# A Mamba-2 mixer on one core: the gates' SiLU ordered behind a group's exponentials, the samples' states in three spread steps

## The chip, the cores and the metric

The kernel runs on one core of a Trainium2 chip. The metric is device time in microseconds (us): the median of three runs before the change is 1595.83 us (1595.36 to 1596.58). A core has five engines that work side by side and wait for one another through semaphores: PE (matrix products, with PEld for its weight loads), DVE (vector), ACT (functions such as exp, SiLU and square root, and scaled copies), POOL (a second, slower vector engine) and SP, which here issues all DMA transfers. Each engine works through its own list of instructions in order: whatever waits at the head of a list holds up all that stands behind it.

## The reference

One step of a two-layer decoder for a prompt of 512 tokens and, with the same weights, 8 samples of 8 tokens each. The kernel carries both as 512 + 64 = 576 columns. Layer 0 is a convolution and window attention mixer, layer 1 a Mamba-2 mixer; each is followed by a gated feed-forward network (FFN). What matters here is the second mixer:

```python
z, xbc, dt = jnp.split(h @ w_in, [D_INNER, D_INNER + SSM_CONV_DIM], axis=-1)
xbc = jax.nn.silu(causal_dwconv(padded, conv_w, conv_b))
...
dt = jax.nn.softplus(dt.astype(jnp.float32) + dt_bias.astype(jnp.float32))
a = -jnp.exp(a_log.astype(jnp.float32))
y, new_ssm = ssd_scan(xs, dt, a, bm, cm, ssm_hist)
y = (y + d_skip[:, None] * xs).reshape(b, t, D_INNER) * jax.nn.silu(z)
y = rmsnorm(y.reshape(b, t, SSM_GROUPS, gs), gn_g.reshape(SSM_GROUPS, gs)).reshape(b, t, D_INNER)
return y @ w_out, new_conv, new_ssm
```

`ssd_scan` works on 32 heads in 4 groups of 8. Within a chunk of 128 tokens it weighs pairs of tokens by exponentials of differences of a running sum (the "decays"), and from chunk to chunk it carries a state. The samples start from given states (`state_ssm`): each of the 8 samples adds what its state gives to its outputs (`y_off`), and returns its state, decayed and with its own tokens added (`h_final`).

## The kernel before

The program is written as straight code over tiles of 128 rows. A scheduler that runs when the kernel is built sets the order on each engine; it may move instructions past one another where the data allow it. Two calls bind it: `keep_in_program_order(m)` keeps a matmul right where the program has it behind the one before, and `issue_after(ins)` keeps what is issued inside its block behind `ins` on the same engine.

**Large products.** Every product with a weight is made of three (L160, L161, L162): weights and activations are split into a high and a low part, and high x high, low x high and high x low are summed. A matmul has 288 columns, half of 576. Weights come by DMA into `wr` (3 buffers, 512 KB each, L141), ACT copies the high part `wh` (L150), DVE subtracts to get the low part `wl` (L151). Results go to PSUM tiles `mm`, of which there are 3 in this mixer.

**The second mixer** (`mix1`) runs `ssd(g)` for groups g = 0 to 3. `ssd` is a generator: at each of its `yield`s the function `run` may emit one item of the list `side`, so that large products lie between the group's own small ones. For g = 0 the side list holds the projections of z for this group (`z_units`, results to `zs`) and of B and C of the next. For g = 1 and 2 it holds the output projection of group g - 1 (`ot`, 8 tiles, activations `yh`/`yl`, in the text "y products") and then z. For g = 3 it holds z first, then four of the eight output tiles of group 2; the other four follow the group.

**Inside a group.** For each chunk c a state is made: a product `pst` (L990), summed into `hst` on DVE (L995, L996); the last goes out (L1000, `out_ssm_p`). Then, for each t = 0 to 3 (two heads each): `carried(t)` loads `ea2` (L1030) and takes its exponential (L1031); `decays` loads `acb` (256 KB, L1017), takes four ReLUs and one Exp on ACT (L1021, L1022), and a product with `cbm` on DVE (L1023); `outputs(t)` runs eight products into `yp` (L1047) from the two `acb`, and two DVE operations (L1051, L1052). After t = 1 and t = 3 comes `samples(bh)` for four samples: it loads four states `h0` (256 KB each, L1060), runs four products `pyo` (L1064), each with 32 output rows, into one PSUM tile, and one DVE operation makes `yo` (L1066); then for each sample a product `pst` (L1071), a scaling of `h0` on POOL (L1072), a sum on DVE (L1075) and the store (L1076). At the group's end `ysp` (L1095, L1100) joins the samples' parts.

**The gate.** `gate(g)` applies SiLU to the four `zs` tiles (L1119), multiplies, sums squares, takes 1/sqrt by way of PE, ACT and DVE (`rstd`, L182 to L197), scales (L1127) and splits into `yh`/`yl` (L170, L171), which the next group's side list, or after g = 3 the last output projection, uses. Exp, SiLU and Sqrt need different tables on ACT; where the next function's table isn't loaded, an ACT_TABLE_LOAD stands ahead of it.

**Memory slots.** Nearly all tiles come from one list of equal slots (48, and 9 more from the first FFN on). `S` takes the slot that was freed first in the program, `free` appends. A tile's DMA therefore waits until the last user of that slot is done, whoever that is. `zs` takes four slots at the start of a group, `prev` (the y tiles of the group before) are freed after `gate`, and `self.h` (16 slots) at the end of the mixer.

In the profile and in the lists of instructions, numbers at the end of a tile's name are left out: `h<-in_h` is `h0` read from memory, `ea` is `ea2`, `x` and `b` in a row of `pst` are `x3` and `b3`.

Of the kernel before, what the change touches and what calls it, by code (L numbers as in the profile page):

```python
# [22 lines left out]
HALF = (slice(0, HB), slice(HB, T))  # L23
# [26 lines left out]

class Builder:
    NSLOT = 48
    EXTRA = 9

    def __init__(self, nc, tc, d, stack):
        self.nc, self.tc, self.d = nc, tc, d
# [718 lines left out]
    def mix1(self):  # L775
        nc, d = self.nc, self.d
# [53 lines left out]
        W = 160  # L830
# [14 lines left out]
        nc.vector.scalar_tensor_tensor(e, v, -1.0, v, op0=MUL, op1=MAX)  # L845
        nc.scalar.activation(e, e, AF.Exp, scale=-1.0)
# [67 lines left out]
        def ssd(g):  # L914
# [18 lines left out]
            b3 = []  # L933
# [80 lines left out]
            def decays(r):  # L1014

                acb = self.S("acb", NP)
                nc.sync.dma_start(acb, acd[8 * g + r, 0:NP].partition_broadcast(P))  # L1017
                for c in range(4):
                    cs = slice(c * P, (c + 1) * P)
                    o = c * 32 + 8 * g + r  # L1020
                    nc.scalar.activation(acb[:, cs], acb[:, cs], AF.Relu, bias=ac[:, o:o + 1], scale=-1.0)  # L1021
                nc.scalar.activation(acb, acb, AF.Exp, scale=-1.0)  # L1022
                nc.vector.tensor_tensor(acb, acb, cbm[:, :NP], op=MUL)  # L1023
                return acb

            def carried(t):

                ea2 = self.S("ea2", NP - P)
                for hh in range(2):
                    nc.sync.dma_start(ea2[hh * 64:hh * 64 + 64, :], acd[8 * g + 2 * t + hh, P:NP].partition_broadcast(64))  # L1030
                nc.scalar.activation(ea2, ea2, AF.Exp)  # L1031
                py = self.ps("py")
                for c in range(1, 4):
                    nc.tensor.matmul(py[:, (c - 1) * P:c * P], H[c - 1][:, t * P:(t + 1) * P], cf[:, c * P:(c + 1) * P],
                                     start=True, stop=True)
                nc.vector.tensor_tensor(ea2, ea2, py[:, 0:NP - P], op=MUL)
                return ea2

            def outputs(t, ea2, pair):

                yp = self.ps("yp", "yp")
                for c in range(4):
                    cs = slice(c * P, (c + 1) * P)
                    for hh in (1, 0):
                        r = 2 * t + hh
                        rows, ch = slice(hh * 64, hh * 64 + 64), slice(r * 64, r * 64 + 64)
                        m = nc.tensor.matmul(yp[rows, cs], xdt[c][:, ch], pair[hh][:, cs], start=True, stop=True)  # L1047
# [7 lines left out]
            def samples(bh):  # L1055

                h0 = []
                for b4 in range(4):
                    h0.append(self.S("h0", NP))
                    nc.sync.dma_start(h0[-1], d["h0"][4 * bh + b4, g])  # L1060
                pyo = self.ps("pyo", "pyo")
                for b4 in range(4):
                    b = 4 * bh + b4
                    nc.tensor.matmul(pyo[b4 * 32:b4 * 32 + 32, :], cf[:, NP + 8 * b:NP + 8 * b + 32], h0[b4], start=True, stop=True)  # L1064
                o = self.S("yo", NP)
                nc.vector.tensor_tensor(hp(o), hp(pyo), eax[:, bh * 32 + 8 * g:bh * 32 + 8 * g + 8].unsqueeze(2).broadcast_to([P, 8, 64]), op=MUL)  # L1066
                yo.append(o)
                for b4 in range(4):
                    b = 4 * bh + b4
                    pst = self.ps("pst")  # L1070
                    nc.tensor.matmul(pst, b3[bh][:, b4 * P:(b4 + 1) * P], x3[bh], start=True, stop=True)  # L1071
                    nc.gpsimd.tensor_tensor(hp(h0[b4]), hp(h0[b4]),  # L1072
                                            cds[:, b * 32 + 8 * g:b * 32 + 8 * g + 8].unsqueeze(2).broadcast_to([P, 8, 64]),
                                            op=MUL)
                    nc.vector.tensor_tensor(h0[b4], h0[b4], pst, op=ADD)  # L1075
                    nc.sync.dma_start(d["ssm_s"][b, g], h0[b4])  # L1076
                    self.free(h0[b4])
# [26 lines left out]
            self.free(bf, cf, cbm, xdt, H, es, yo)  # L1104

        def z_units(g):
            zss[g] = [self.S("zs") for _ in range(4)]

            def evac(t):
                return lambda half, p: nc.scalar.activation(zss[g][t][:, HALF[half]], p[:, :HB], AF.Copy)  # L1110
            return [(d["w_in_o"][4 * g + t], P, evac(t)) for t in range(4)]

        def gate(g, yv):

            zs = zss.pop(g)
            ssq, rs = self.S("gssq"), self.S("grs")
            ys = [self.pair("y") for _ in range(4)]
            for t in range(4):
                nc.scalar.activation(zs[t], zs[t], AF.Silu)  # L1119
# [22 lines left out]
        def single(units):  # L1142
            return [lambda u=u: self.units([u], 1) for u in units]

        ys = None
        for g in range(4):
            xs = xss[g]
            side = []
            zu = z_units(g)
            if g:  # L1150
                ws = {}
                prev, srcs = ys, [d["w_out_o"][g - 1, c] for c in range(4)]

# [8 lines left out]
                side = single(zu) + ot[:4] if g == 3 else ot + single(zu)  # L1162
# [7 lines left out]
            if g:  # L1170
                self.free(prev)
# [180 lines left out]
```

## Time and profile before

| | us |
|---|---|
| median of three runs | 1595.83 (1595.36 to 1596.58) |
| profiled execution, its own time | 1596.65 |
| its span, first to last instruction | 1594.9 |
| PE busy in the span | 1560.2 (98%) |
| DVE busy | 999.7 (63%) |
| ACT busy | 656.1 (41%) |
| POOL busy | 149.4 (9%) |

The page's "busy" of PE is the time in which at least one matmul is in flight; matmuls overlap, so a row's duration (0.29 us for a matmul of 288 columns) is longer than the distance to the next one's start. For what a matmul costs in a dense stream the distance between starts is read. "Idle before" is the time an engine stood still ahead of an instruction, with the engine or DMA that ended it. The clock column (PEclk) is the TensorE clock that was granted, as a share of full speed.

### The profile page before, as it was taken

The numbers are of one execution on the slowest core, as the hardware profiler recorded it, in microseconds if no ns is written. First come the engines' busy times: TensorE is split into PE (matmuls) and PEld (weight loads), VectorE is DVE, ScalarE is ACT, GpSimd is POOL, SyncE is SP. The second block draws the span as 40 slices with busy tenths as digits, with TensorE's granted clock in tenths as the row PEclk, the third lists the DMA queues.
The fourth block names the chain that finished last, engine by engine and source line by source line (L and its number), as shares of the span: only waits on it lengthen the run. The fifth ranks groups of instructions, "written<-read, shape, count | busy, mean of one in ns | idle before, by whom it ended". The sixth has DMA issues, their size and how long they took to land.

```text
span 1594.9 us, 28738 instructions
## 1 busy us (share of the span) xinstructions
PE 1560.2 (98%) x11709; PEld 1479.2 (93%) x11709; DVE 999.7 (63%) x1750; ACT 656.1 (41%) x1210; POOL 149.4 (9%) x362
## 2 busy tenths in 40 slices
PE   8999999999999999999999999999999999999999
PEld 8976799999999999998987987998899999999999
DVE  7958486663564464678885686676776643663552
ACT  6257363321232222479654655556443221221220
POOL 0026001000000000101202101101110000000000
PEclk9999999999999999999999999999999999999999
DMA  7514223222222222226245226235222232223222
GB/s 229 117 54 102 70 83 101 80 81 92 80 77 84 93 80 75 74 82 203 74 120 186 74 81 195 89 96 182 81 89 84 80 91 83 80 73 97 83 82 76
DMA packets 69841, 157.60 MB, mean 99 GB/s; under 512 B 20158, under 2 KB 24510, under 8 KB 69710
## 3 DMA queue, kind: packets, MB, share of 16 engines
q1 hardware_dynamic: 69710, 155.77, 31.9%
q8 instruction: 92, 1.51, 0.4%
q14 instruction: 39, 0.32, 0.1%
HBM read 140.54 MB, written 15.21 MB: 98 GB/s over the span
## 4 chain that ended last, share of the span: by engine, by line
PE 82%; DVE 7%; ACT 4%; DMA 4%; issue 1%; POOL 1%; SPq 0%; ACTq 0%; DVEq 0%; POOLq 0%
PE mm L160 24%; PE mm L161 24%; PE mm L162 24%; DMA acb<-acd 2%; DVE cconv L801 1%; PE mm L559 1%; PE yp L1047 1%; DMA h<-in_h 1%; PE pyo L1064 1%; PE pt L182 1%; DVE ca L436 1%; ACT wh L150 1%; DVE wl L151 1%; ACT acb L1021 1%; PE pr L193 1%
## 5 line engine op out<-in xcount | busy, mean ns | idle before, releaser
L160 PE MATMUL mm<-hh,wh 128*128 128x288 f32 (+1 forms) x2288 | 682.8, 299 | 8.4 <-ACT wh L150 7.7
L161 PE MATMUL mm<-hl,wh 128*128 128x288 f32 (+1 forms) x2288 | 678.6, 297 | 0.0
L162 PE MATMUL mm<-hh,wl 128*128 128x288 f32 x2288 | 677.6, 296 | 0.0
L150 ACT ACTIVATE wh<-wr 128x1024 fp32r<-128x1024 f32 (+1 forms) x215 | 223.4, 1039 | 541.0 <-PE mm L161 273.6
L160 PEld LDWEIGHTS mm<-hh,wh 128*128 128x128 f32 (+1 forms) x2288 | 429.8, 188 | 14.9 <-ACT wh L150 7.9
L161 PEld LDWEIGHTS mm<-hl,wh 128*128 128x128 f32 (+1 forms) x2288 | 430.2, 188 | 5.6 <-issue 3.8
L162 PEld LDWEIGHTS mm<-hh,wl 128*128 128x128 f32 x2288 | 430.7, 188 | 2.7 <-issue 1.3
L151 DVE TENSOR_TENSOR wl<-wr,wh 128x1024 fp32r<-128x1024 f32 (+1 forms) x215 | 259.2, 1206 | 77.5 <-ACT wh L150 77.3
L160 PE MATMUL mm<-yh,wh 128*128 128x288 f32 x960 | 286.8, 300 | 2.2 <-ACT yh L170 2.2
L161 PE MATMUL mm<-yl,wh 128*128 128x288 f32 x960 | 288.2, 300 | 0.1
L162 PE MATMUL mm<-yh,wl 128*128 128x288 f32 x960 | 284.8, 297 | 1.4 <-DVE wl L151 1.4
L162 PEld LDWEIGHTS mm<-yh,wl 128*128 128x128 f32 x960 | 181.6, 189 | 6.1 <-issue 4.1
L161 PEld LDWEIGHTS mm<-yl,wh 128*128 128x128 f32 x960 | 181.9, 189 | 5.3 <-issue 4.0
L160 PEld LDWEIGHTS mm<-yh,wh 128*128 128x128 f32 x960 | 181.5, 189 | 4.4 <-ACT yh L170 2.6
L259 DVE TENSOR_TENSOR x<-x,mm 128x288 f32<-128x288 f32 x192 | 85.4, 450 | 157.4 <-PE mm L162 157.2
L304 DVE TENSOR_TENSOR gbuf<-mm,rs 128x224 f32<-128x224 f32 x44 | 17.2, 391 | 108.0 <-PE mm L162 108.0
L315 ACT ACTIVATE gsilu<-gconv,par 128x512 f32<-128x512 f32 x44 | 31.8, 723 | 115.5 <-DVE gconv L312 115.5
L312 DVE SCALAR_TENSOR_TENSOR gconv<-gbuf,par,gconv 128x592 f32<-128x592 f32 x88 | 73.1, 831 | 1.5
L325 DVE TENSOR_TENSOR gsilu<-mm,gsilu 128x288 f32<-128x288 f32 x88 | 40.0, 454 | 49.7 <-PE mm L162 49.7
L801 DVE SCALAR_TENSOR_TENSOR cconv<-cbuf,par,cconv 128x600 f32<-128x600 f32 x72 | 61.5, 857 | 13.0 <-ACT cconv L799 12.0
L307 POOL COPY fpo<-gbuf 128x2 f32<-128x2 f32 x44 | 12.4, 281 | 497.6 <-DVE gbuf L304 497.6
L1072 POOL TENSOR_TENSOR h<-h,cds 128x512 f32<-128x512 f32 x32 | 36.7, 1166 | 186.5 <-PE pyo L1064 167.8
(306 smaller groups left out, 1640.9 us busy)
## 6 DMA issues: line engine op xcount, KB each, us to landing
wr<-in_w_gate SPq DMA_DIRECT2D x44, 512.0 KB, 3.3
wr<-in_w_up SPq DMA_DIRECT2D x44, 512.0 KB, 3.3
wr<-in_w_in_o SPq DMA_DIRECT2D x40, 512.0 KB, 3.5
wr<-in_w_down SPq DMA_DIRECT2D x32, 448.0 KB, 3.4
wr<-in_w_down SPq DMA_DIRECT2D x16, 512.0 KB, 3.5
acb<-acd SPq DMA_DIRECT2D x32, 256.0 KB, 3.9
h<-in_h SPq DMA_DIRECT2D x32, 256.0 KB, 3.5
out_ssm_s<-h SPq DMA_DIRECT2D x32, 256.0 KB, 2.1
```

What stands on the lines that cost most here:

```text
L150: nc.scalar.activation(hi[:, :n], raw[:, :n], AF.Copy)
L151: nc.vector.tensor_tensor(lo[:, :n], raw[:, :n], hi[:, :n].bitcast(F32), op=SUB)
L160: nc.tensor.matmul(out, hi[:, ws], xh[:, sl], start=i == 0, stop=False)
L161: nc.tensor.matmul(out, hi[:, ws], xl[:, sl], start=False, stop=False)
L162: nc.tensor.matmul(out, lo[:, ws], xh[:, sl], start=False, stop=i == n - 1)
L259: nc.vector.tensor_tensor(self.x[m][:, sl], self.x[m][:, sl], p[:, :HB], op=ADD)
L304: nc.vector.tensor_tensor(g[:, 290:514], p[:, 0:224], rs[:, HB:NP], op=MUL)
L312: nc.vector.scalar_tensor_tensor(cv[:, :592], g[:, k:592 + k], w(k), cv[:, :592], op0=MUL, op1=ADD)
L315: nc.scalar.activation(sl[:, :NP], cv[:, :NP], AF.Silu, bias=b)
L325: nc.vector.tensor_tensor(sl[:, HALF[half]], p[:, :HB], sl[:, HALF[half]], op=MUL)
L801: nc.vector.scalar_tensor_tensor(cv[:, :600], g[:, k:600 + k], w(k), cv[:, :600], op0=MUL, op1=ADD)
L1072: nc.gpsimd.tensor_tensor(hp(h0[b4]), hp(h0[b4]), cds[:, b * 32 + 8 * g:b * 32 + 8 * g + 8].unsqueeze(2).broadcast_to([P, 8, 64]), op=MUL)
```

## The change

Four edits, all but the first three lines in `mix1`.

- **Samples in three steps.** `samples` becomes `load(bh)` (the four loads of `h0`), `begin(bh)` (the four `pyo` products, kept in one run, the last sample's first; all four scalings on POOL; `yo`) and `finish(bh, behind)` (the four `pst`, kept behind the last `yp` product of the t at hand, the sums and the stores). `load(0)` stands ahead of t = 0, `begin(0)` after t = 0, `finish(0)` after t = 1, `load(1)` right behind it, `begin(1)` after t = 2, `finish(1)` after t = 3.
- **SiLU behind the exponentials.** The gate's four SiLU are issued behind the group's last Exp of `decays`.
- **Slots.** 11 extra slots for 9 (five small tiles of the softplus become slots that are freed); `zs` takes its slot when its first half is written; `prev` is freed when the eighth output tile is issued; in the last group `self.h` is freed as soon as the z projections have used it.

```diff
-    EXTRA = 9
+    EXTRA = 11
...
-        v = self.Z("sp_v", W, bufs=1)
+        v = self.S("sp_v", W)
...
-        e, z, z2, q = (self.Z(n_, W, bufs=1) for n_ in ("sp_e", "sp_z", "sp_z2", "sp_q"))
+        e, z, z2, q = (self.S(n_, W) for n_ in ("sp_e", "sp_z", "sp_z2", "sp_q"))
...
+        self.free(v, e, z, z2, q)
...
-                nc.scalar.activation(acb, acb, AF.Exp, scale=-1.0)
+                self.last_exp = nc.scalar.activation(acb, acb, AF.Exp, scale=-1.0).ins
...
+                return m.ins
+
+            h0 = {}
+
+            def load(bh):
+                h0[bh] = []
                 for b4 in range(4):
-                    h0.append(self.S("h0", NP))
-                    nc.sync.dma_start(h0[-1], d["h0"][4 * bh + b4, g])
+                    h0[bh].append(self.S("h0", NP))
+                    nc.sync.dma_start(h0[bh][b4], d["h0"][4 * bh + b4, g])
+
+            def begin(bh):
                 pyo = self.ps("pyo", "pyo")
+                for b4 in (3, 2, 1, 0):
+                    b = 4 * bh + b4
+                    m = nc.tensor.matmul(pyo[b4 * 32:b4 * 32 + 32, :], cf[:, NP + 8 * b:NP + 8 * b + 32], h0[bh][b4],
+                                         start=True, stop=True)
+                    if b4 < 3:
+                        self.tc.keep_in_program_order(m)
                 for b4 in range(4):
                     b = 4 * bh + b4
-                    nc.tensor.matmul(pyo[b4 * 32:b4 * 32 + 32, :], cf[:, NP + 8 * b:NP + 8 * b + 32], h0[b4], start=True, stop=True)
+                    nc.gpsimd.tensor_tensor(hp(h0[bh][b4]), hp(h0[bh][b4]),
+                                            cds[:, b * 32 + 8 * g:b * 32 + 8 * g + 8].unsqueeze(2).broadcast_to([P, 8, 64]),
+                                            op=MUL)
...
+            def finish(bh, behind):
                 for b4 in range(4):
                     b = 4 * bh + b4
                     pst = self.ps("pst")
-                    nc.tensor.matmul(pst, b3[bh][:, b4 * P:(b4 + 1) * P], x3[bh], start=True, stop=True)
...
+                    with self.tc.issue_after(behind):
+                        nc.tensor.matmul(pst, b3[bh][:, b4 * P:(b4 + 1) * P], x3[bh], start=True, stop=True)
+                    nc.vector.tensor_tensor(h0[bh][b4], h0[bh][b4], pst, op=ADD)
+                    nc.sync.dma_start(d["ssm_s"][b, g], h0[bh][b4])
+                    self.free(h0[bh][b4])
...
             for t in range(4):
+                if t == 0:
+                    load(0)
                 ea2 = carried(t)
...
-                outputs(t, ea2, pair)
+                last = outputs(t, ea2, pair)
                 yield
                 if t % 2:
-                    yield from samples(t // 2)
+                    yield from finish(t // 2, last)
+                    if t == 1:
+                        load(1)
+                else:
+                    begin(t // 2)
...
-            for t in range(4):
-                nc.scalar.activation(zs[t], zs[t], AF.Silu)
+            with self.tc.issue_after(self.last_exp):
+                for t in range(4):
+                    nc.scalar.activation(zs[t], zs[t], AF.Silu)
...
+                    if m == 7:
+                        self.free(prev)
...
+                def last_h():
+                    self.free(self.h)
+                    self.h = []
+                side = single(zu) + [last_h] + ot[:4] if g == 3 else ot + single(zu)
```

The scheduler then makes new lists. On PE and ACT they are the same as before up to the mixer's first group and again in the second FFN; in the FFNs POOL's small fills and copies stand in a somewhat different order. What lies between is ordered anew. Line numbers behind L833 move: L1064 becomes L1070, L1071 becomes L1089, L1047 L1048, L1022 L1023, L1119 L1145, L1060 L1063, L1017 L1018, L1000 L1001, L1005 L1006.

**PE, the second group's t = 3 before, with its second four samples.** Before, two of the four `pyo` stand here and the other two 27 and 34 rows further on, each alone among large products:

```order
L1064 MATMUL pyo<-h_9493,cfm 32x512
L1064 MATMUL pyo<-h_9495,cfm 32x512
L1071 MATMUL pst<-x_8868,b_8849 128x512 x2
L160 MATMUL mm<-hh,wh 128x288
L161 MATMUL mm<-hl,wh 128x288
L162 MATMUL mm<-hh,wl 128x288
L1047 MATMUL yp<-acb,xdt 64x128 x8
L1071 MATMUL pst<-x_8868,b_8849 128x512
```

Now, the same four samples' products ahead of the `yp` of t = 2:

```order
L162 MATMUL mm<-hh,wl 128x288
L1070 MATMUL pyo<-h_9307,cfm 32x512
L1070 MATMUL pyo<-h_9305,cfm 32x512
L1070 MATMUL pyo<-h_9303,cfm 32x512
L1070 MATMUL pyo<-h_9301,cfm 32x512
L1048 MATMUL yp<-acb,xdt 64x128 x8
L1035 MATMUL py<-cfm,hst 128x128 x3
```

All eight sets of four `pyo` now stand as one run. Before, only the two of the first group did: the list had 18 runs in all. The eight `yp` products of a t, split as 1 and 7 at two places before, are whole everywhere. In the last group, the large y products that are left between the last `yp` and the end of the output tiles are 112 now; they were 64.

**SP, the second group from its exponentials' loads on.** Before:

```order
L1005 DMA es<-acd 64x8x64
L1030 DMA ea_9074<-acd 64x384 x2
L1017 DMA acb<-acd 128x512 x2
L1030 DMA ea_9172<-acd 64x384 x2
L1017 DMA acb<-acd 128x512
L1000 DMA out_ssm_p<-hst 128x512
L141 DMA wr<-in_w_in_o 128x1024
L1017 DMA acb<-acd 128x512
L1060 DMA h_9244<-in_h 128x512
L1060 DMA h_9242<-in_h 128x512
```

Now, from the third load of a sample's state (two more stand right ahead of it):

```order
L1063 DMA h_9076<-in_h 128x512
L1031 DMA ea_9078<-acd 64x384 x2
L1018 DMA acb<-acd 128x512
L1006 DMA es<-acd 64x8x64
L1063 DMA h_9070<-in_h 128x512
L141 DMA wr<-in_w_in_o 128x1024
L1018 DMA acb<-acd 128x512
L1031 DMA ea_9187<-acd 64x384 x2
L1018 DMA acb<-acd 128x512
L1063 DMA h_9301<-in_h 128x512
L1001 DMA out_ssm_p<-hst 128x512
L1018 DMA acb<-acd 128x512
```

The states' loads moved ahead of the decays' loads, and those of the second four samples to either side of the `acb` that stands behind the store of the chunk's state. That `acb` (the fourth of the group) takes the slot of the stored `hst` in both lists and so waits for that store to land.

**ACT, the third group's last exponentials.** Before:

```order
L1022 ACTIVATE acb<-acb 128x512
L1119 ACT_TABLE_LOAD
L1119 ACTIVATE zs<-zs 128x576
L1021 ACTIVATE acb<-acb,ac 128x128 x4
L1110 ACTIVATE zs<-mm 128x288
L1022 ACT_TABLE_LOAD
L1022 ACTIVATE acb<-acb 128x512
L1110 ACTIVATE zs<-mm 128x288
```

Now:

```order
L1022 ACTIVATE acb<-acb,ac 128x128 x2
L1134 ACTIVATE zs<-mm 128x288
L1022 ACTIVATE acb<-acb,ac 128x128 x2
L150 ACTIVATE wh<-wr 128x1024
L1023 ACTIVATE acb<-acb 128x512
L1145 ACT_TABLE_LOAD
L1145 ACTIVATE zs<-zs 128x576
L1134 ACTIVATE zs<-mm 128x288
```

The two table loads between the last two Exp are gone; one stands behind the last Exp. Over the program there are 36 table loads, 49 before.

More of the change, by code (lines that the diff above doesn't have):

```diff
@@ L1053, in outputs @@
                 self.free(pair, ea2)
-            def samples(bh):
-                h0 = []
+                return m.ins
+            h0 = {}
+            def load(bh):
+                h0[bh] = []
                 for b4 in range(4):
-                    h0.append(self.S("h0", NP))
-                    nc.sync.dma_start(h0[-1], d["h0"][4 * bh + b4, g])
+                    h0[bh].append(self.S("h0", NP))
+                    nc.sync.dma_start(h0[bh][b4], d["h0"][4 * bh + b4, g])
+            def begin(bh):
                 pyo = self.ps("pyo", "pyo")
+                for b4 in (3, 2, 1, 0):
[4 more added lines that the diff above has]
+                        self.tc.keep_in_program_order(m)
                 for b4 in range(4):
                     b = 4 * bh + b4
-                    nc.tensor.matmul(pyo[b4 * 32:b4 * 32 + 32, :], cf[:, NP + 8 * b:NP + 8 * b + 32], h0[b4], start=True, stop=True)
+                    nc.gpsimd.tensor_tensor(hp(h0[bh][b4]), hp(h0[bh][b4]),
+                                            cds[:, b * 32 + 8 * g:b * 32 + 8 * g + 8].unsqueeze(2).broadcast_to([P, 8, 64]),
+                                            op=MUL)
                 o = self.S("yo", NP)
@@ L1070, in samples @@
                     pst = self.ps("pst")
[L1071 to L1077, printed above, removed]
+                    with self.tc.issue_after(behind):
[3 more added lines that the diff above has]
+                    self.free(h0[bh][b4])
                     if b4 % 2:
@@ L1106, in z_units, with go @@
         def z_units(g):
-            zss[g] = [self.S("zs") for _ in range(4)]
+            zss[g] = []
             def evac(t):
-                return lambda half, p: nc.scalar.activation(zss[g][t][:, HALF[half]], p[:, :HB], AF.Copy)
+                def go(half, p):
+                    if half == 0:
+                        zss[g].append(self.S("zs"))
+                    nc.scalar.activation(zss[g][t][:, HALF[half]], p[:, :HB], AF.Copy)
+                return go
             return [(d["w_in_o"][4 * g + t], P, evac(t)) for t in range(4)]
@@ L1160, in out_tile @@
                         self.add_x(m, hf, p)
+                    if m == 7:
+                        self.free(prev)
                 ot = [lambda m=m: out_tile(m) for m in range(8)]
-                side = single(zu) + ot[:4] if g == 3 else ot + single(zu)
+                def last_h():
+                    self.free(self.h)
+                    self.h = []
+                side = single(zu) + [last_h] + ot[:4] if g == 3 else ot + single(zu)
             else:
@@ L1169, in mix1 @@
                     f()
-            if g:
-                self.free(prev)
             if g < 3:
```

## The prediction

> **What bounds the kernel now.** I read the page first, then stages, then what PE waits for.
>
> ```profile
> PE 1560.2 (98%) x11709; PEld 1479.2 (93%) x11709; DVE 999.7 (63%) x1750; ACT 656.1 (41%) x1210; POOL 149.4 (9%) x362
> ```
>
> PE is the bound; no other engine comes near. So a change pays only by what it takes out of PE's stream or its gaps. The windows, by stage (the four groups of the second mixer from 686 to 1150, then a stretch of the last FFN):
>
> ```profile
> core 0: us, PE busy (x) PEld busy (x) DVE busy (x) ACT busy (x) POOL busy (x), PEclk, DMA share, GB/s
> 686.00:807.00 121.00, 117.88 (x897) 108.91 (x897) 95.66 (x160) 91.80 (x192) 20.64 (x40) 1.00 0.38 120
> 807.00:931.00 124.00, 119.13 (x872) 106.89 (x871) 85.79 (x143) 69.37 (x143) 16.86 (x33) 1.00 0.39 121
> 931.00:1055.00 124.00, 119.44 (x882) 108.04 (x881) 86.32 (x144) 69.23 (x144) 16.46 (x33) 1.00 0.38 120
> 1055.00:1150.00 95.00, 89.92 (x626) 77.50 (x625) 69.02 (x126) 49.59 (x101) 12.21 (x16) 0.96 0.43 135
> 1300.00:1400.00 100.00, 100.00 (x758) 100.00 (x757) 46.86 (x71) 22.13 (x28) 3.06 (x18) 1.00 0.27 85
> ```
>
> PE is idle for 3.1, 4.9, 4.6 and 5.1 us in the four groups, 17.6 us together. In the FFN it never is: 758 matmuls in 100 us, so a large one costs 0.132 us. What follows the mixer therefore starts sooner by all that the mixer loses, and gives nothing back. PE's waits that lie in the mixer:
>
> ```profile
> PE yp L1047 <- DVE acb L1023: 5.6, 7, 1.3
> PE pyo L1064 <- DMA h<-in_h: 3.4, 3, 1.7
> PE mm L160 <- ACT yh L170: 2.2, 1, 2.2
> PE ysp L1095 <- DVE yo L1066: 1.6, 1, 1.6
> PE mm L162 <- DVE wl L151: 1.4, 1, 1.4
> PE pst L1071 <- DVE ea L1036: 0.8, 1, 0.8
> PE pst L1071 <- DVE h L1075: 0.8, 2, 0.5
> ```
>
> These make 15.8 of the 17.6 us; the rest are waits of a few tenths for small steps that the change leaves alone.
>
> **Term 1, the pinned runs.** The timeline of PE shows `pyo` four at a time (x8, since each of these matmuls is two rows) and one at a time (x2), with the next start behind it:
>
> ```profile
> 741.89 1.06 PE L1064 MATMUL pyo<-h,cfm 128*32 128x512 f32 x8
> 742.89 0.51 PE L1071 MATMUL pst<-x,b 96*128 96x512 f32 x1
> 1126.34 1.04 PE L1064 MATMUL pyo<-h,cfm 128*32 128x512 f32 x2
> 1127.31 0.40 PE L162 MATMUL mm<-yh,wl 128*128 128x288 f32 x1
> ```
>
> Four together take 1.00 us from start to start, one alone 0.97 us: products into different 32-row strips run at once when they are neighbours. Before there are 18 runs (the first and the last are shown), 17.6 us at 0.98; after, 8 runs of 1.00 us. That is **-9.6 us**, all on PE and independent of any wait.
>
> **Term 2, whole `yp` runs.** Two of the sixteen are split 1 and 7. The single one costs the distance to the next start:
>
> ```profile
> 834.96 0.43 PE L1047 MATMUL yp<-acb,xdt 128*64 128x128 f32 x2
> 835.32 0.40 PE L160 MATMUL mm<-yh,wh 128*128 128x288 f32 x1
> ```
>
> 0.36 us each, while the other seven still take the time of a full run. **-0.7 us.**
>
> **Term 3, waits that go.** `pyo` on its DMA, 3.4 us: the states' loads now stand ahead of the decays' loads and no longer behind the stores of the four samples before; to zero. `ysp` on `yo`, 1.6 us: `yo` of the second four is made after t = 2 and has a whole t (48 large products, 6.3 us) as cover; to zero. `pst` on `h` and `ea`, 1.6 us: POOL's scalings are done ahead, so the sum on DVE that frees PSUM waits for nothing; to 0.4. `mm` on `yh`, 2.2 us:
>
> ```profile
> 1138.34 0.40 PE L160 MATMUL mm<-yh,wh 128*128 128x288 f32 x1 [2.22 <-ACT yh L170]
> L1119 ACT ACTIVATE zs<-zs 128x576 f32<-128x576 f32 x16 | 11.0, 685 | 0.3
> ```
>
> In the last group 112 large products (14.8 us) now lie behind the last `yp`, where there were 64 (8.4 us). So 6.4 us of cover come in where 2.2 were short. The SiLU now wait for the last Exp; with one table load (1.28 us) and four of 0.69 us they take 4.0 us of ACT, while DVE has to multiply the decay, PE to run `yp` and DVE to add it. Were none of that beside them, the 4.0 us would still be less than the new cover. Behind them on ACT stand the gate's squares and the casts of the next weights, for which PE has three buffers. `mm` on `wl`, 1.4 us: an accident of DVE's order, half of it. Sum **-9.1 us**.
>
> **Term 4, waits for `acb`: no gain.** Two things feed them. One is a table load between ReLU and Exp, in the chain of waits at the third group's last `yp`:
>
> ```profile
> 982.12 3.99 DMA acb<-acd
> 986.22 1.28 ACT acb L1021 x4
> 987.81 1.28 ACT L1022
> 989.10 0.64 ACT acb L1022
> 989.77 1.41 DVE acb L1023
> 991.23 1.12 PE yp L1047 x16
> ```
>
> `ACT L1022` of 1.28 us is the load; PE stood 1.3 us there, and 0.7 us at the same place of the second group:
>
> ```profile
> 866.60 1.09 PE L1047 MATMUL yp<-acb,xdt 128*64 128x128 f32 x16 [0.72 <-DVE acb L1023]
> ```
>
> These 2.0 us go. The other eleven loads that go (11 x 1.28 = 14 us of ACT) lie beside PE's work. The second feed is the slot of `hst`, here from the fourth state's `pst` (822.70) on:
>
> ```profile
> 822.70 0.59 PE L990 MATMUL pst<-xde,btok 128*128 128x512 f32 x1
> 825.57 4.05 DMA out_ssm_p<-hst
> 829.64 5.31 DMA acb<-acd
> 835.03 1.29 ACT acb L1021 x4
> 836.34 0.64 ACT acb L1022
> 837.01 0.70 DVE acb L1023
> 837.76 1.09 PE yp L1047 x14
> ```
>
> The store must land before the fourth `acb` may load: 12.2 us from the store to `yp`, in the second group and, by SP's same order, in the third. This stays, but its cover shrinks. After the fourth state's `pst` PE's new list has, up to that `yp` in the second group: the `pst` 0.86, two `py` 0.66, 56 large products 7.4, `pyo` 1.0, a `yp` 1.0: 10.9 us, for 15.1 us before (822.70 to 837.76, with 2.0 us of waiting in it). The store started 2.9 us behind that `pst`; 16 large products now stand ahead of it, in which DVE, which was behind with the states' sums, catches up, so I take 1.7. Then `yp` is ready at 13.9 us: a wait of 3.0. With the shortest landing of an `acb` (3.3 us for 5.3, and a store 1 us quicker) nothing is left of it; with the states' loads in flight beside it, it may be a whole landing longer:
>
> ```profile
> h<-in_h SPq DMA_DIRECT2D x32, 256.0 KB, 3.5
> ```
>
> that is 6.5. I take 2.3 us for each of the two groups, on the near side of the row because the second `acb` of 982 landed in 3.99, and 1 us each for `yp` of t = 2 in the second group (its `acb` waits behind four stores on SP) and for the last group (two y-sets between its last `yp`, 4 us, against 3.8 us of ACT for two `acb`). So 5.6 us of old waits, of which 2.0 are gone for certain, give way to 6.6: **+1.0 us**.
>
> **Term 5, the clock.** Windows around the 2.2 us wait:
>
> ```profile
> 1136.30:1139.73 3.43, 1.29 (x7) 1.08 (x8) 3.35 (x9) 2.99 (x8) 0.00 (x0) 1.00 0.00 0
> 1139.73:1146.56 6.83, 6.83 (x33) 6.83 (x32) 4.52 (x11) 1.88 (x5) 0.00 (x0) 0.50 0.22 77
> ```
>
> PE was busy for 1.29 of 3.43 us, and then had half its clock for 6.83 us: 33 matmuls where 0.132 us each would be 4.4 us. If the wait goes, so does this: **-2.4 us**. [...] So I keep the term, and count in the range that a new wait may cost 2.4 us again.
>
> **The sum.** -9.6 - 0.7 - 9.1 + 1.0 - 2.4 = -20.8 us. Against the profiled execution's own 1596.65 (span 1594.9) that is 1575.9; the median shown is 0.8 lower than that execution, so I predict **1575 us**. Edits at nothing: the small softplus tiles and the two slots by themselves; POOL's four scalings in a row (about 4 us), behind which only small fills stand, which PE reaches a group later; `pst` kept behind `yp`, which only keeps it off PE's queue until PSUM is free, and would cost at most the 0.4 us left in term 3.
>
> **Rivals.**
> *The waits only change places.* SP is one queue: eight states' loads ahead of the decays make each `acb` later, and PE waits for `acb` what it waited elsewhere. For it: the two chains above are DMA time for the most part. Against: more slots are free, so fewer loads wait for one. Then only terms 1 and 2 hold: 1596.65 - 10.3 - 0.8 = 1585.5.
> *Clean.* The landings are short and the new waits vanish: 6.6 us less, 1568.
> *Slower: the pinned run at the head of PE's queue.* A run of four can't start before its last state has landed, and all large products stand behind it. A state takes 3.5 us to land (the row above). Should each of the 8 runs wait that long, 28 us come in where term 3 has nothing: 1595.8 - 20.8 + 28 = 1603. It decides from 20.8 / 8 = 2.6 us per run, and can be told from no change from 3.0. Against it: by SP's new order most states are issued a whole t ahead of their run.
> *The runs don't overlap.* In reverse order the four could run one after another: 8 x 4 x 0.98 = 31.4 for 8.0, so 1598. `yp`, in reverse order too, does overlap (the 16 rows at 866.60 take 1.09 us), so this is unlikely.
>
> **How the numbers follow.** Forecast (1571 to 1580) 0.52; places changed (1580 to 1591) 0.25; clean (1565 to 1571) 0.15; pinned run 0.05; no overlap 0.03. The range takes the forecast, most of the second case and half of the third: 1568 to 1588. A measurement tells about 0.2% (3 us) from no change; the last two cases and a small tail of the second give slower 0.05 and same 0.03, the rest is faster, 0.92.
>
> **What would show it.** Right: 8 runs of `pyo` x8 about 1.0 us each; no PE wait for `h`, `yo` or `yh`; the clock at 1.00 behind the last group; 36 table loads; PE's idle time in the mixer near 10 us, most of it at `yp` on `acb` in the second and third group. Wrong: `pyo` with idle time on a DMA, idle time at `yp` above 8 us, or a window at half clock behind one of them.

## The result, and the profile after

The changed kernel takes **1579.41 us** (median of four runs, 1577.22 to 1581.55) against 1596.05 for the kernel before, a ratio of 0.9902 (95% interval 0.9886 to 0.9918): 16.6 us less. 1575 was predicted, 1568 to 1588 as the range. The profiled executions differ by 16.5 us of span. The page's first part, and the waits of PE, which answer to the rows of before (what waited, for what, then us in total, times, longest):

```profile
span 1578.4 us, 28672 instructions
PE 1547.4 (98%) x11709; PEld 1478.0 (94%) x11709; DVE 997.7 (63%) x1750; ACT 642.0 (41%) x1197; POOL 146.9 (9%) x362
```

```profile
PE yp L1048 <- DVE acb L1024: 7.9, 4, 2.7
PE pst L1089 <- DVE ea L1037: 1.7, 1, 1.7
PE mm L160 <- DVE x L259: 1.0, 2, 0.7
PE pt L950 <- ACT r L929: 1.0, 1, 1.0
PE pst L1089 <- DVE h L1090: 0.4, 1, 0.4
PE mm L162 <- DVE wl L151: 0.4, 1, 0.4
```

The rows for `h`, `yo` and `yh` (3.4, 1.6 and 2.2 us before) are gone, and PE is busy for 12.8 us less (1560.2 to 1547.4): 9.6 of these are the `pyo` products (17.7 to 8.0 from start to next start), which now share their time, 1.2 the `yp` products and 1.9 the large ones. The waits at `yp` are fewer (7 before, 4 now) but longer. On PE's timeline (start, length, instruction, count, idle time before it), a `pyo` run and two of those waits:

```profile
841.10 1.09 PE L1048 MATMUL yp<-acb,xdt 128*64 128x128 f32 x16 [2.68 <-DVE acb L1024]
...
855.00 1.07 PE L1070 MATMUL pyo<-h,cfm 128*32 128x512 f32 x8
857.78 1.09 PE L1048 MATMUL yp<-acb,xdt 128*64 128x128 f32 x16 [1.71 <-DVE acb L1024]
```

The others are 1.60 us (at 958) and 1.92 us (at 1088). The clock in windows around the two longest (us, then PE busy and its matmuls, PEld, DVE, ACT, POOL, then the granted clock):

```profile
839.18:842.59 3.41, 1.49 (x18) 1.27 (x19) 2.23 (x4) 1.11 (x3) 0.00 (x0) 1.00 0.59 193
842.59:846.00 3.41, 3.41 (x16) 3.30 (x15) 2.65 (x5) 0.00 (x0) 0.00 (x0) 0.50 0.57 95
...
1088.35:1091.76 3.41, 1.49 (x19) 1.09 (x19) 1.81 (x3) 3.41 (x10) 1.56 (x2) 1.00 0.71 237
1091.76:1095.17 3.41, 3.41 (x13) 3.10 (x13) 2.31 (x4) 3.41 (x11) 0.00 (x0) 0.50 0.28 110
```

Before there was one stretch of 6.83 us at half clock in the mixer; now there are two of 3.41 us, the same total, behind two of the new waits.

### The profile page after: what moved, and what is told of

Read it like the earlier page. It is cut to its first block, busy times and chain, and to the rows that moved or that the text cites. A ratio compares the mean times of both kernels' runs of the same rounds, so it can differ in the third digit from the quotient of the medians.

```text
span 1578.4 us, 28672 instructions
## 1 busy us (share of the span) xinstructions
PE 1547.4 (98%) x11709; PEld 1478.0 (94%) x11709; DVE 997.7 (63%) x1750; ACT 642.0 (41%) x1197; POOL 146.9 (9%) x362
## 5 line engine op out<-in xcount | busy, mean ns | idle before, releaser
L304 DVE TENSOR_TENSOR gbuf<-mm,rs 128x224 f32<-128x224 f32 x44 | 17.2, 391 | 108.9 <-PE mm L162 108.9
L1022 ACT ACTIVATE acb<-acb,ac 128x128 f32<-128x128 f32 x128 | 41.4, 390 | 50.6 <-DMA acb<-acd 34.4
L307 POOL COPY fpo<-gbuf 128x2 f32<-128x2 f32 x44 | 12.4, 281 | 476.0 <-DVE gbuf L304 476.0
```

The lines of the kernel that those rows point to most:

```text
L304: nc.vector.tensor_tensor(g[:, 290:514], p[:, 0:224], rs[:, HB:NP], op=MUL)
```

## Experiments

Three sets of runs, each with the kernel before on the same chip, whose medians were 1595.82 (e1 to e4), 1596.50 (e5 to e8) and 1593.80 us (e9 to e12); so ratios are compared. The last three columns are from the one profiled execution of each: runs of `pyo` on PE, PE's idle time from 686 to 1170 us (484 us less PE's busy time in that window), and windows of 3.41 us at half clock in it. The windows differ between executions of one kernel (two in after, one in e8, which is the same kernel), so a difference of one or two says little.

| kernel | median us | ratio to before (95%) | `pyo` runs | PE idle | half-clock windows |
|---|---|---|---|---|---|
| before | 1596.05 | 1 | 18 | 17.7 | 2 |
| after | 1579.41 | 0.9902 (0.9886 to 0.9918) | 8 | 13.4 | 2 |
| e1 pins alone | 1614.53 | 1.0107 (1.0087 to 1.0128) | 11 | 31.3 | 9 |
| e2 after, no pins | 1579.12 | 0.9895 (0.9879 to 0.9911) | 10 | 11.2 | 3 |
| e3 SiLU order alone | 1597.22 | 1.0009 (0.9999 to 1.0019) | 16 | 17.0 | 2 |
| e4 after, slots swapped | 1572.87 | 0.9860 (0.9845 to 0.9875) | 8 | 9.2 | 1 |
| e5 after, no SiLU order | 1577.47 | 0.9889 (0.9864 to 0.9914) | 9 | 11.4 | 0 |
| e6 slots and SiLU order | 1575.59 | 0.9876 (0.9857 to 0.9895) | 11 | 7.9 | 1 |
| e7 e4, later loads | 1575.84 | 0.9875 (0.9852 to 0.9899) | 8 | 11.0 | 1 |
| e8 after, once more | 1579.58 | 0.9901 (0.9882 to 0.9921) | 8 | 12.6 | 1 |
| e9 all slot edits alone | 1581.95 | 0.9919 (0.9905 to 0.9934) | 11 | 9.5 | 3 |
| e10 two slots alone | 1582.44 | 0.9920 (0.9907 to 0.9934) | 10 | 11.3 | 4 |
| e11 early give-backs alone | 1590.26 | 0.9974 (0.9964 to 0.9984) | 14 | 12.4 | 3 |
| e12 e4, no SiLU order | 1575.07 | 0.9875 (0.9858 to 0.9892) | 9 | 11.2 | 1 |

### Which part pays: e1, e2, e3

**e1**, the pinned run alone, at its old place in the kernel before:

```diff
-                for b4 in range(4):
+                for b4 in (3, 2, 1, 0):
                     b = 4 * bh + b4
-                    nc.tensor.matmul(pyo[...], ..., h0[b4], start=True, stop=True)
+                    m = nc.tensor.matmul(pyo[...], ..., h0[b4], start=True, stop=True)
+                    if b4 < 3:
+                        self.tc.keep_in_program_order(m)
```

> The kernel before, with one edit: the four pyo products of a run are written in descending order and pinned together, everything else at its old place. In program order the 32 products then stand in 11 runs in place of 18. Theory (each run costs about 1.0 us whatever it holds): 18 x 0.98 = 17.6 us becomes 11 x 1.0 = 11.0, so 1596.0 - 6.6 = 1589.4 us, with the PE's wait for h at its 3.4 us or a little more, since the pinned run waits for the last of its four loads. Rival (what pays is the earlier load and the spread steps, not the pin): the pinned runs wait for their h for as long as they save, 1595 to 1597 us, with idle PE before pyo near 10 us.

Both sides were wrong: some 18 us slower. The runs did shrink, but a new wait came in. PE's waits, then the timelines of PE, DVE and POOL:

```profile
PE pst L1073 <- DVE h L1077: 15.9, 11, 2.8
```

```profile
851.63 1.07 PE L1064 MATMUL pyo<-h,cfm 128*32 128x512 f32 x8 [0.55 <-DMA h<-in_h]
...
855.58 0.51 PE L1073 MATMUL pst<-x,b 96*128 96x512 f32 x1 [1.10 <-DVE h L1077]
...
857.58 0.50 PE L1073 MATMUL pst<-x,b 96*128 96x512 f32 x1 [1.09 <-DVE h L1077]
```

```profile
854.84 0.69 DVE L1077 TENSOR_TENSOR h<-h,pst 128x512 f32<-128x512 f32 x1 [1.31 <-POOL h L1074]
```

```profile
852.76 4.05 POOL L1074 TENSOR_TENSOR h<-h,cds 128x512 f32<-128x512 f32 x4 [41.37 <-PE pyo L1064]
```

POOL can't scale a state before its `pyo` has read it. With the four pinned, all four scalings start at the run's end and follow one another at about 1 us. PE's list here has the third `pst` of the four only 12 large products (1.6 us) behind the run and the fourth 3 further on; the sums on DVE, the PSUM that they free and these `pst` go at POOL's pace. PE's idle time grew by 13.6 us, and seven more half-clock windows at about 1.5 us (the hardware section) are 10.5; less 6.9 us for the runs (17.7 to 10.8) that is 17.2 of the 20.2 us between the two spans. This execution also has two more such windows ahead of the mixer (at 189 and 196 us); at the same price they would be the rest.

A run of four with its row on POOL is not enough for this. At the same place e6 (below) has both without a pin, but 22 large products between the second `pst` and the third, and none of them waits (PE's timeline, then POOL's):

```profile
841.62 0.73 PE L1072 MATMUL pst<-x,b 96*128 96x512 f32 x2
...
845.10 0.85 PE L1072 MATMUL pst<-x,b 96*128 96x512 f32 x2
```

```profile
841.75 4.40 POOL L1073 TENSOR_TENSOR h<-h,cds 128x512 f32<-128x512 f32 x4 [32.80 <-PE pyo L1065]
```

So what costs is how soon behind the run the list has its `pst`. The spread steps, which let POOL scale a whole t ahead, are one way to make that room.

**e2**, the change without the pins:

```diff
-                for b4 in (3, 2, 1, 0):
+                for b4 in range(4):
...
-                    if b4 < 3:
-                        self.tc.keep_in_program_order(m)
```

> The kernel after, without the pins and with the four pyo products in ascending order. In program order they stand in 10 runs in place of 8. Theory (a run costs 1.0 us): +2.0 us, 1581.4 us, no wait for h. Rival (the overlap needs the pinned descending order): products of a run follow one another at 0.97 us each, 32 x 0.97 = 31 us in place of 8, near 1602 us.

The time is that of the kernel after; the products overlap unpinned and in ascending order too. Two more runs cost 2 us, which is within what the interval leaves. The pin is not what joins the runs: without it there are 10, for 18 before.

**e3**, the SiLU order alone, in the kernel before:

```diff
-                nc.scalar.activation(acb, acb, AF.Exp, scale=-1.0)
+                self.last_exp = nc.scalar.activation(acb, acb, AF.Exp, scale=-1.0).ins
...
-            for t in range(4):
-                nc.scalar.activation(zs[t], zs[t], AF.Silu)
+            with self.tc.issue_after(self.last_exp):
+                for t in range(4):
+                    nc.scalar.activation(zs[t], zs[t], AF.Silu)
```

> The kernel before, with one edit: a gate's four SiLU stand behind the group's last exponential. Theory of the prediction: the 2.0 us of waits at yp that came from table loads go, and no other term: 1594.0 us, 13 table loads fewer. If the wait of 2.2 us ahead of the half-clock window at 1139 us goes too, its 2.4 us go with it: 1591.6. Rival (table loads were never on the path): 1596 us, with the idle time of the PE in the mixer as before, 17.6 us.

In time the rival holds: ACT has 36 table loads in place of 49, and nothing is gained. But the waits at `yp` did fall, from 5.6 to 2.8 us, more than the theory says; they came back at `pst`, which had 1.6 us before:

```profile
PE pst L1071 <- DVE h L1075: 2.9, 4, 1.8
PE yp L1047 <- DVE acb L1023: 2.8, 4, 1.0
PE pst L1071 <- DVE ea L1036: 2.4, 1, 2.4
```

### What pays instead: e6, e9, e10, e11

**e6** keeps `samples` as it was, in one step, with the other edits of the change.

> The kernel after with the samples' states as they were before (one step, no pins), so the SiLU ordering and the slot edits alone. Theory (the spread steps carry the gain, slots only make room for them): 1595 to 1597 us, pyo at 14 to 18 runs, idle PE in the mixer near 16 us. Rival (slots given back earlier are worth something alone, since loads start earlier): 1590 us or less.

**e9** takes the SiLU order out of e6 as well:

> The kernel before with the slot edits alone (11 extra slots, early give-backs, slots of z taken late); neither the SiLU ordering nor the spread, pinned samples. Theory (after e3 and e6: the slots carry the whole gain): as e6, 1575 to 1577 us, pyo in 11 runs, idle PE in the mixer near 7.6 us. Rival (e6 owes part of it to the SiLU ordering, whose table loads matter only once the h loads are early): 1578 to 1582 us.

**e10** is the kernel before with two more slots (and the softplus tiles moved into slots to make the room):

```diff
-    EXTRA = 9
+    EXTRA = 11
```

> The kernel before with two more slots and nothing else (11 extra, their room taken from the five tiles of the softplus, which become slots). In program order pyo stands in 10 runs in place of 18. Theory (two slots more let the h loads start early): 18 to 10 runs is -7.8 us and the wait for h of 3.4 us goes, 1596.2 - 11.2 = 1585.0 us or less. Rival (two slots are used up at once, only the early give-backs help): 1592 to 1597 us.

**e11** has the early give-backs (`prev`, `self.h`) and the late `zs`, but 9 extra slots:

> The kernel before with the early give-backs and the late z slots, without the two extra slots. In program order pyo stands in 14 runs in place of 18. Theory (each part of the slot edits gives its share): -4 us for the runs and up to 3.4 us for the wait for h, 1589 to 1592 us. Rival (the give-backs alone do it): 1575 to 1580 us.

e6's theory fell outright. Without the new steps the time is 0.9876 of before, and so not above after's 0.9902 (the intervals just overlap). Two slots alone give 0.9920, which is 12.8 us of 1596 and four fifths of the whole change. The scheduler then places the four products side by side by itself (18 runs to 10), and PE's waits for `h` shrink from 3.4 us to one of 1 us, which hides inside a run of 2.07 us (weight loads of PE):

```profile
845.65 0.14 PEld L1065 LDWEIGHTS pyo<-h,cfm 128*32 128x32 f32 x4 [0.95 <-DMA h<-in_h]
```

It is not that the loads of `h` find free slots: on SP they still wait for theirs (33.5 us in all in the mixer, 37.1 before). But more slots also change which tile gets which slot, and the one behind the store of the chunk's state now goes to a load of `h` in place of an `acb` (SP's waits before, then in e10):

```profile
SPq L1017 <- DMA out_ssm_p<-hst: 9.3, 3, 4.6
```

```profile
SPq L1061 <- DMA out_ssm_p<-hst: 9.5, 3, 3.4
```

So how much of e10's gain is room, and how much is the changed order, isn't separated; no run changes the order alone in the kernel before. The give-backs alone give 0.9974, and on top of the two slots nothing (0.9919).

e9's rival held as to size, since the SiLU order is worth 0.43% on top of the slots (0.9876 against 0.9919, in two sets of runs; the intervals are apart). But at the place where the two differ most, table loads are not how. In e9, DVE's list has a multiplication of `acb` ahead of the sums; it waits for ACT, and PE for the sum behind it (PE's timeline, then DVE's):

```profile
752.76 0.51 PE L1072 MATMUL pst<-x,b 96*128 96x512 f32 x1 [3.59 <-DVE h L1076]
```

```profile
749.13 1.06 DVE L1024 TENSOR_TENSOR acb<-acb,cbm 128x512 f32<-128x512 f32 x1 [2.80 <-ACT acb L1023]
```

That ACT work waited for a load of `acb`, not for a table (ACT's timeline):

```profile
747.29 1.28 ACT L1022 ACTIVATE acb<-acb,ac 128x128 f32<-128x128 f32 x4 [2.25 <-DMA acb<-acd]
```

In e6 DVE's list has the sums ahead of the multiplications, and PE's wait for a sum is short (DVE's timeline, then PE's waits):

```profile
749.38 2.77 DVE L1076 TENSOR_TENSOR h<-h,pst 128x512 f32<-128x512 f32 x4
752.07 1.29 DVE L1024 TENSOR_TENSOR acb<-acb,cbm 128x512 f32<-128x512 f32 x2
```

```profile
PE pst L1072 <- DVE h L1076: 1.4, 1, 1.4
```

So the order moved the scheduler's list, here to the better: 2.2 us of wait, and two half-clock windows fewer in those executions (about 3 us). That this is chance is argued, not shown; e5 and e12 below speak for it.

### The order's worth in the full change: e5, e12

> The kernel after, with the gates' SiLU no longer ordered behind the last exponential. In program order the pyo products stand in 9 runs in place of 8. Theory of the prediction (table loads cost 2.0 us of waits at yp): 49 table loads in place of 36, 1579.4 + 2.0 + 1.0 = 1582.4 us. Rival, after e3 (the table loads are beside the path): 1579.4 to 1580.4 us.

The predicted loss did not come; 0.9889 and 0.9902 overlap. **e12** is the same removal in e4:

> e4 without the SiLU ordering. In program order pyo stands in 9 runs in place of 8. Theory (the SiLU ordering is worth nothing, as e3 and e5 say): 1572 to 1575 us, like e4. Rival (the ordering pays once acb is no longer late for another reason): 2 us or more above e4, 1575 to 1578 us.

0.9875 against e4's 0.9860, again overlapping. By the medians the order's sign changes with the list around it, but neither difference is told apart from none; that it has a worth of its own isn't shown.

### The new wait at `yp`, and the clock: e4, e7, e8

**e4** changes one line of the kernel after:

```diff
-            self.free(H.pop(), btok)
+            self.free(btok, H.pop())
```

> The kernel after, with one edit: btok's slot is given back ahead of the slot of the stored state, so that the slot that waits for the store of out_ssm_p goes to an h load and not to the fourth acb. Theory A (the new waits at yp are that acb behind that store, and the lower clock is their sequel): the idle time before yp at 838 us (2.68) and at 958 us (1.60) goes, and the half-clock window at 842.6 to 846.0 with it (about 1.2 us): 1579.4 - 5.5 = 1573.9 us. Rival B (the sync engine's queue is held up by whichever load takes the slot, and the acb loads behind it come as late): 1578 to 1581 us, waits at yp and both half-clock windows as they are. Rival C: the waits go, and the clock falls as before: 1575.1.

Theory A: 1572.87 us, the fastest of all, and apart from after (0.9845 to 0.9875 against 0.9886 to 0.9918). SP's queue after, then in e4:

```profile
827.65 0.43 SPq L1063 DMA_DIRECT2D h<-in_h  x1
828.43 0.34 SPq L1001 DMA_DIRECT2D out_ssm_p<-hst  x1
834.40 0.32 SPq L1018 DMA_DIRECT2D acb<-acd  x1
834.82 2.23 SPq L1063 DMA_DIRECT2D h<-in_h  x3
```

```profile
826.64 0.81 SPq L1018 DMA_DIRECT2D acb<-acd  x2
827.80 0.34 SPq L1001 DMA_DIRECT2D out_ssm_p<-hst  x1
833.34 2.91 SPq L1063 DMA_DIRECT2D h<-in_h  x4
838.14 0.33 SPq L1018 DMA_DIRECT2D acb<-acd  x1
```

SP stands still behind the store as long as before (5.6 and 5.2 us), but both `acb` have gone ahead, and what waits is `h`, which PE needs a whole t later. PE's waits at `yp` fall from 7.9 to 3.0 us:

```profile
PE yp L1048 <- DVE acb L1024: 3.0, 3, 1.9
```

The half-clock window at 842.6 is gone, and so is that at 1091.8, although its wait of 1.93 us stayed. One came at 746.6, though, behind a 1.73 us wait that had none in after (1.74 us at 745.6), which no theory of the length of a wait explains:

```profile
743.22:746.63 3.41, 1.68 (x12) 1.40 (x11) 3.32 (x5) 1.00 (x2) 2.36 (x2) 1.00 0.39 144
746.63:750.04 3.41, 3.41 (x14) 3.21 (x14) 1.99 (x4) 1.91 (x5) 0.00 (x0) 0.50 0.61 230
```

**e7** moves `load(1)` behind the second t-step's first two decays, for the last group's wait:

```diff
                     pair.append(decays(2 * t + hh))
+                    if t == 2 and hh:
+                        load(1)
...
-                    if t == 1:
-                        load(1)
```

> e4 with one more edit: the second half's h loads are written behind the decays of the third step in place of ahead of them, so that in the last group the acb loads stand ahead of them on the sync engine's queue. Theory (the last group's 1.92 us wait at yp is acb behind the h loads on that queue): this wait goes, 1572.9 - 1.9 = 1571.0 us, and 1.2 to 1.7 us less where its half-clock window goes too. Rival (the h loads are late in turn): the PE waits for h ahead of pyo of the second half by 2 us or more a group, 1573 to 1580 us.

Neither: 1575.84 lies where the rival put it, but 0.9875 is not told apart from e4, and what the rival gave as the reason, 2 us or more of waits for `h`, did not come (0.18 us in all). The last group's wait only went from 1.93 to 1.65 us; and in the second group the pattern of e9 returned (PE, then DVE):

```profile
846.73 0.50 PE L1089 MATMUL pst<-x,b 96*128 96x512 f32 x1 [2.68 <-DVE h L1090]
```

```profile
844.55 0.69 DVE L1024 TENSOR_TENSOR acb<-acb,cbm 128x512 f32<-128x512 f32 x1 [3.07 <-ACT acb L1023]
```

**e8** is the kernel after, unchanged:

> The kernel after, unchanged, profiled once more. Grid theory (the clock is set for windows of 3.41 us on a grid that runs on whatever the kernel does, to a half where the PE was busy for under about half of the window before): the same waits at yp within 0.1 us, but half-clock windows behind other waits or none, always whole multiples of 3.413 us apart, each behind a window with a busy share under 0.51, and none behind one over 0.62. Rival (the length of a wait alone decides, so 1.92 us drops the clock and 1.74 does not): the same two windows within 0.2 us of 842.6 and 1091.8 us, and no other in the mixer.

The same wait at 838 us, and one half-clock window in the mixer, at another phase; none behind 1088, where the same 1.93 us wait now lies across two windows of the grid:

```profile
837.60:841.01 3.41, 0.95 (x8) 0.72 (x6) 1.26 (x2) 1.91 (x5) 0.00 (x0) 1.00 0.93 297
841.01:844.42 3.41, 3.26 (x20) 2.74 (x21) 3.17 (x6) 0.00 (x0) 0.00 (x0) 0.50 0.19 61
...
1086.80:1090.20 3.40, 1.80 (x14) 1.56 (x12) 2.14 (x5) 3.40 (x11) 3.12 (x3) 1.00 0.99 276
1090.20:1093.62 3.42, 3.09 (x29) 2.80 (x30) 2.82 (x6) 3.42 (x12) 0.00 (x0) 1.00 0.19 77
```

For these two the grid theory's numbers were right: PE was busy for 0.28 of the window at 837.60 us, and one at half clock follows; for 0.53 of that at 1086.80, and none follows. Its bound of 0.62 is not general: in e1, ahead of the first FFN, a half-clock window follows one in which PE was busy throughout (the hardware section).

## Why the prediction came near, and which of its steps failed

The time came within its range and 4.4 us from the centre. Of its signs of being right, the runs, the waits that go and the 36 table loads came; PE's idle time in the mixer was 13.4 us, not near 10. Of its signs of being wrong, one came: a half-clock window behind a wait at `yp`, twice; the idle time at `yp` stopped at 7.9 us, just short of its 8. By its own steps:

- **Term 1 (-9.6 us): right in size, wrong in cause.** Eight runs of 1.00 us each. But the prediction credits the pin, and puts "the two slots by themselves" among the edits at nothing. That step failed: e10 shows that two slots give 10 runs and 0.9920, e2 that leaving the pin out of the full change costs no time that can be told, e1 that by itself it costs 18 us. The term was read off the new list on PE, which shows what happens and not which edit does it.
- **Term 2 (-0.7).** Sixteen whole `yp` runs of 1.02 us, from start to next start, are 16.3, for 17.6 before: -1.3. The two splits are 0.7 of it, as said; the rest is a third run (at 1089.62 us), which was whole in the list but took 1.60 us with a short wait inside.
- **Term 3 (-9.1): sizes.** The five waits sum to 10.2 before. `h`, `yo` and `yh` are at zero as said; `wl` kept 0.4 for 0.7; but `pst` has 2.1 where 0.4 was left. So -7.7, and two small waits nobody had named grew (`mm` on `x` by 0.7, `pt` on `r` by 0.5).
- **Term 4 (+1.0): mis-sized.** 5.6 to 7.9 us is +2.3. The mechanism was right, as e4 shows, but the two waits behind the store were 2.7 and 1.6 for 2.3 each, and the single us put on the second group's t = 2 and on the last group were 1.7 and 1.9. That the wait "stays" was a matter of one line. And the 2.0 us of old waits that were "gone for certain" are no gain by themselves: in e3 they go, and more comes back at `pst`.
- **Term 5 (-2.4): did not come.** This is the largest miss. The 2.2 us wait went with its half-clock stretch, but two new waits brought two windows, 6.83 us again. The prediction held this only as a possibility in the range; a term for a clock that follows waits has to be worked out for the waits that come as well. Part of the miss is the draw of one execution: e8, the same kernel, had one window in the mixer and was 1.5 us shorter (1578.68 for 1580.21).

Sum of the differences: 2.4 (clock) + 1.4 (term 3) + 1.3 (term 4) + 1.2 (small waits) - 0.6 (term 2) = 5.7 of less gain; the measured gap to the forecast, -20.8 against -16.4 in the profiled executions' own times, is 4.4. The other 1.3 us is a term that the prediction left out: a large product right behind another kind of matmul takes 0.22 us to the next start (median in the mixer) in place of 0.13, and after has 130 such places for 145. By an estimate from these, 15 x 0.09 us.

Of the rivals, "places changed" was half true (three quarters of the idle time stayed, under other names); "pinned run at the head of PE's queue" did not show in after, but e1 shows its cousin, with POOL instead of a DMA at the other end.

What each edit is worth, then: the slot edits alone give most of the gain; the SiLU order and the steps with their pins shift which wait is longest, and with both in place the result is no better than without the steps. With the slot order of e4 the steps cost nothing any more; whether they gain anything over e6 isn't told apart (0.9860 and 0.9876). Two kernels were not run: the steps without the slot edits, which might join the runs by themselves, and e6 with the slot order of e4, which would say whether the steps are needed at all. e4 has the lowest median, but e5, e6, e7 and e12 are not told apart from it.

## What to carry to other kernels

Where tiles share one list of slots, test the number and order of the slots first: two more slots, which also change which tile gets which, moved more time here than any order written by hand, and swapping two names in one `free` moved 6.5 us. A load that waits for a slot holds up the whole queue behind it (SP stood still for 5.6 us in after, behind one store), so give the slot whose last user is a store to the tile that is needed last. And where a change has several edits, a term read off the combined list must not be credited to the edit that names it: take each alone, in the kernel before.

## What the runs showed of the hardware

**The clock changed on a grid.** In the profiles of before and after the half-clock windows begin at whole multiples of 3.413 us from one another (before: 0, 288.0 and 421.0 windows from the first, at 156.69 us; after: 0, 201.0, 274.0 and 417.0 from 156.51 us). Against the program the phase can differ: the window behind the wait at 838 us begins at 842.59 us in after and at 841.01 in e8, the same kernel. Of the 278 windows of the two grids in the mixer (686 to 1170 us) that were themselves at full clock, the three with PE busy for 0.38 to 0.44 of it (1136.32 in before, 839.18 and 1088.35 in after) were followed by one at half clock; the six with 0.55 to 0.62 and the 269 with 0.64 or more were not. Of the windows shown above, 0.28 (e8) and 0.49 (e4) were followed by one, 0.53 (e8) was not. At which share it turns isn't shown. Nor does this hold outside the mixer: at the end of after a window with 0.48 (1573.04 us) was followed by full clock, and ahead of the first FFN, in e1, one in which PE was busy without a gap by half:

```profile
185.97:189.38 3.41, 3.41 (x35) 3.41 (x35) 2.17 (x6) 2.59 (x6) 0.00 (x0) 1.00 0.00 0
189.38:192.79 3.41, 3.41 (x17) 3.41 (x16) 0.75 (x3) 2.17 (x5) 0.00 (x0) 0.50 0.00 0
```

So PE's busy share, as the profile shows it, is not all that decides. In a half-clock window large products start 0.24 us apart, not 0.132:

```profile
843.02 0.44 PE L161 MATMUL mm<-yl,wh 128*128 128x288 f32 x1
843.26 0.44 PE L162 MATMUL mm<-yh,wl 128*128 128x288 f32 x1
```

so one costs 3.41 x (1 - 0.132 / 0.24) = 1.5 us. In the mixer a wait can thus cost 1.5 us more, or not, by where the grid falls: one of 1.73 us did in e4, one of 1.74 us in after and one of 1.93 us in e8 did not. That may be a part of the spread between runs of one kernel, up to 7 us for the kernel before. What keeps the second window of a stretch like the 6.83 us at half clock isn't settled.

**A run of `pyo` costs the same with one product or four** (0.97 and 1.00 us at full clock in before), pinned and descending (1.00 in after) or not (1.00 in e6), if all four states are there; the run of e10 whose last state landed within it took 2.07 us.
